# A gather's scaled sums moved from the vector engine to matmuls in column quarters

## The chip, the cores and the metric

The kernel runs on one core of a Trainium2 chip. The metric is the time of a launch on the device in microseconds (us), the median of several runs. The profiler's own execution is told by its span, from the first instruction to the last.

## The reference, cut to what matters

Two layers work on 256 latent tokens and 256 context tokens of 1024 features. A layer mixes tokens (a chunked gated delta rule whose latent scan starts from the context's final state, a pooling mixer, a Fourier mixer), and then looks up experts:

```python
# PEER: 8 heads, 128 x 128 experts, 16 chosen per head and token
s_top, i_top = top_k(scores, 16)                 # by each of two halves of a key
best, pos = top_k(sums of pairs, 16)
idx  = key_0 * 128 + key_1                       # 8 x 16 = 128 experts of a token
gate = softmax(best)
act  = gelu(sum_d h[t, d] * expert_u[idx[t, k], d])
out[t] = sum_k gate[t, k] * act[t, k] * expert_v[idx[t, k]]
x = x + g2 * out
```

The last layer needs of the context only the states of its scans. So experts are looked up three times: for the context in the first layer, and for the latents in both. All data are float32.

## The kernel before, in words

The program is written in Python, unrolled, and handed to a planner that gives each of the engines a fixed order of instructions: what comes earlier in the program has priority, and an instruction that is ready may pass one that is not. Tiles come from pools with a tag and a number of buffers; a new tile of a tag waits until the one whose place it takes has been read for the last time. PSUM's eight banks are tags as well (`BANKS`, line 173): "pj0", "pj1", "c0", "c1", "c2", "s" once each and "po" twice. `using(...)` gives a stage other tags.

The order of the program is: modulation vectors; the context's columns, scan and update in the first layer; the choice of the context's experts (`gather_select`, line 910); a first part of fetching their rows (`gather_rows`, line 956); the latents' columns, scan, update and choice in the first layer; the latents' experts in the first layer (`stream`, line 1087); the last layer for the latents, which ends with a second `stream`.

The latents' lookups are dense. `stream` goes over 128 first keys. For each, `first(i)` loads a tile of u, splits it in two parts (ACT's copy, line 1100, and POOL's subtraction, line 231, called from 1101) and adds 24 matmuls of 128x256 to a bank "s" (lines 1111 to 1113); `second(i)`, 17 tiles behind, weights the activations with the gates, splits a tile of v, and adds 12 matmuls of 128x512 to four banks (line 1142). In the first layer the gates of 32 first keys at a time are built by `chunk` (line 1028): one-hot tiles on DVE, 768 small matmuls (line 1052), copies to SBUF.

The context's lookup is a gather. `gather_select` writes a head's 16 indices per token as soon as that head is chosen (line 939), tokens on partitions. `gather_rows` takes choice j of block b of 128 tokens: an indirect DMA from POOL's queue (line 966) brings for each token, on its own partition, one row of a table that holds u and v side by side, 2048 numbers or 8 KB. DVE multiplies the half of u with the token's features and sums (line 975; 19 of the 256 go to POOL and ACT, lines 972 and 973), ACT applies Gelu and the gate (lines 979 and 980), and DVE adds the half of v, scaled by that one number per token, to the block's sum (line 986):

```python
dve.scalar_tensor_tensor(acc, v, dots[:, i : i + 1], acc, op0=OP.mult, op1=OP.add)
```

The first 100 of 256 such steps stand ahead of the latents' first layer (lines 1193 to 1195) with four buffers of 8 KB for them, the others behind first key 114 of the stream (`KV`, lines 177 and 1239) with three, followed there by the context's residual and its columns and scan of the last layer (`context`, line 1220). Being late in the program, these steps fill in where an engine has nothing of higher priority.

Of the kernel before, what the change touches and what calls it, by code (L numbers as in the profile page):

```python
# [28 lines left out]
def _constants():  # L29
# [4 lines left out]
    # cumulative sums along the tokens of a chunk, forwards and backwards: [j, i]  # L34
# [5 lines left out]
    # masks are added to exponents' arguments: [token, token], nothing outside a chunk  # L40
# [40 lines left out]
def _tiles(w, width):  # L81
    """[1024, n] as [128, n / width, 8 / deep, deep * width], deep * width = 2048: a partition's share of a
    tile lies together, deep rows of 128 in it."""
    deep = 2048 // width
    n = w.shape[1]
    w = w.reshape(KT // deep, deep, 128, n // width, width).transpose(2, 3, 0, 1, 4)
    return np.ascontiguousarray(w.reshape(128, n // width, KT // deep, 2048))


def _columns(v):  # L90
    """[..., 128 n] as [128, ..., n]"""
    v = v.reshape(*v.shape[:-1], -1, 128)
    return np.ascontiguousarray(np.moveaxis(v, -1, 0))


def _layout(i):
# [25 lines left out]
    for l in range(depth):  # L122
# [9 lines left out]
        if l < depth - 1:  # L132
            a[f"uv{l}"] = np.concatenate([i["expert_u"][l], i["expert_v"][l]], 1)
        # a tile per first key: the rows of u transposed, and the rows of v
# [10 lines left out]
def _body(st, tc, a, out, dbg, until):  # L145
# [26 lines left out]
    # the banks of PSUM: three for projections, one for each of three chains, two that sum outputs  # L172
# [3 lines left out]
    KC, TC = 32, 8  # first keys of a chunk of gates, tokens at a time  # L176
    KV = 114
    KVC = 2
    roles = {"ring": None, "split": None, "lo": "pool", "sb": 2, "wb": 1}  # what a stage uses in place of its own tags of PSUM, and of the weights' ring
# [11 lines left out]
    class Stage:  # L191
        """tiles of a pool that is opened and closed by hand"""
# [11 lines left out]
    def bank(shape, tag):  # L204
        tag = roles.get(tag, tag)
        if tag == "pj":
            turns[0] += 1
            tag = f"pj{turns[0] % 2}"
        return pp.tile(shape, F32, tag=tag, bufs=BANKS[tag], name=nm(tag))
# [23 lines left out]
    def rsqrt(x, n, tag=""):  # L233
        """1 / sqrt(x) of [128, n] positive values, by Newton's steps."""
# [10 lines left out]
    def two_parts(x, hi, lo):  # L245
        """x as a sum of two parts that the tensor engine reads exactly in one pass each"""
        act.copy(hi, x)
        (pool_tt if roles["lo"] == "pool" else dve.tensor_tensor)(lo, x, hi.bitcast(F32), op=OP.subtract)
        return hi, lo

    def product(out, x, y, start, stop):
        """out += x^T y, of operands in one part, or in two: only the product of the two second ones drops out"""
# [4 lines left out]
    def wtile(name, *index):  # L257
        """2048 of a weight's columns as two tiles; a function of a row of 128 and the columns' width"""
# [15 lines left out]
    def modulation(l, vecs):  # L274
        """[128, 6, 8, stream]: modulation vectors, a feature per partition."""
        m = mods[l]
        for vec in vecs:
            for half in range(2):
                # quarter j of the partitions sums the rows k = j, j + 4 for the two streams
# [22 lines left out]
    def scales(l, which, m, s):  # L302
        """norm's weight times 1 + scale, and the shift: [128, 8] each"""
# [4 lines left out]
    def in_rows(vec, half, tag):  # L308
        """half of [128, 8] as a row of 512, the same on all partitions"""
# [10 lines left out]
    def normed(x, xn, tag, scratch=None):  # L320
        """xn = x / rms(x), by rows"""
# [7 lines left out]
    def transposed(xns, sc, sh, hT):  # L329
        """hT [128, 8, 256] = (xn * sc + sh) transposed"""  # L330
# [16 lines left out]
    def columns_by_feature(name, c, hs):  # L347
        """256 columns of a weight times hT: [128, 2, 256], a column per partition"""
# [10 lines left out]
    def columns_by_token(name, n, h):  # L359
        """512 columns of a weight times hT: a block's [128, 512] each, a token per partition"""  # L360
# [44 lines left out]
    def columns(l, s, m, full, keep, tl):  # L405
# [4 lines left out]
        else:  # the last use of X  # L410
# [13 lines left out]
        # gates of the delta rule: [token, block, 16]  # L424
# [16 lines left out]
        # softplus(z) = max(z, 0) + ln(1 + exp(-|z|))  # L441
# [24 lines left out]
        # factors by token: [beta, -beta exp(g), exp(g_end - g)]  # L466
# [6 lines left out]
        # decay of a whole chunk, on all partitions: [chunk, 8]  # L473
# [13 lines left out]
        def conv(part, hp):  # L487
            """silu of the short convolution for two heads: part 0, 1, 2 = q, k, v: [128, 2, 256]"""
# [15 lines left out]
        def by_token(part, tok, feat, norm_scale):  # L504
            """a part by token [128, 2, 4, 128] (and by feature [128, 4, 256]), each head's vector over its norm"""
# [39 lines left out]
        if full:  # L545
            # the remaining columns by token: the delta rule's gate | pooling | Fourier
# [63 lines left out]
    def scan(l, s, full, state, tl, chains=4):  # L610
# [9 lines left out]
        def prepare(i):  # L620
# [5 lines left out]
            # g by token, along the columns  # L626
# [21 lines left out]
            # (1 + L)^-1, from blocks of one row on, two blocks at a time  # L648
# [40 lines left out]
        for step in range(4):  # L689
# [3 lines left out]
            for d in range(2):  # L693
# [25 lines left out]
                if full:  # L719
                    # a chunk's bank sums both directions: started once, by its first product  # L720
# [13 lines left out]
    def update(l, s, m, state, po, tl):  # L734
# [3 lines left out]
        # output of the delta rule: normed, gated  # L738
# [27 lines left out]
    def select(l, sp, hs, pair, gates, groups, after=lambda h: None):  # L766
        """pair(h): the keys of a head's chosen experts, [128, block, 2, 16]; gates(h, n): the gates of n heads from
        h on, [128, block, n, 16]; groups: how many heads' gates are worked out at a time"""
# [49 lines left out]
        def by_pair(h, tv, ti):  # L818
            tif = sp("tif", [128, NB * 2, TOPK], 2, BF)
            act.copy(tif, ti.rearrange("p b i k -> p (b i) k"))  # L820
            # of the 16 x 16 sums only those can be chosen that fewer than 16 others precede in both orders:
            # all of rows 0 to 3, and four columns of the others
# [12 lines left out]
            # their rows and columns  # L835
# [19 lines left out]
            # and by those the keys  # L855
# [42 lines left out]
    def residual(l, s, m, accs):  # L898
        """X += g2 * accs, halves of [128, 512] by block"""
# [10 lines left out]
    def gather_select(l, s, m, rows, done):  # L910
        """the chosen experts and gates per token, for their rows to be fetched"""
        idx = rows("idx", [128, NB, HEADS * TOPK], 1, I32)
        gate = rows("gate", [128, NB, HEADS, TOPK])
        st = {}
        for b in range(NB):
            st["acc", b] = rows(f"acc{b}", [128, D])
# [19 lines left out]
        def after(h):  # L936
            if h == 0:
                by_token()
            dve.scalar_tensor_tensor(
                idx[:, :, h * TOPK : h * TOPK + TOPK], keys[0][:, :, 0], float(NKEYS), keys[0][:, :, 1],  # L940
# [3 lines left out]
        keys = [None]  # L944
        select(l, sp, (hT,), pair, lambda h, n: gate[:, :, h : h + n], GROUPS, after)
        for b in range(NB):
            st["h2", b], st["idx", b], st["gate", b] = h2[b], idx[:, b], gate[:, b]
            dump(f"idx{l}{s}{b}", st["idx", b])
            dump(f"gate{l}{s}{b}", st["gate", b])
        sp.close()  # L950
        return st

    GRP = 1
    GROUPS = (1, 2, 5)

    def gather_rows(l, s, m, rows, buffer, st):
        """the chosen experts' rows fetched per token, a group of them for all tokens of a block at a time"""
        for j0 in range(0, HEADS * TOPK, GRP):
            h = j0 // TOPK
            for b in range(NB):  # L960
                acc = st["acc", b]
                dots = rows("dots", [128, GRP], 4)
                uvs = []
                for i in range(GRP):
                    uv = buffer()
                    pool.indirect_dma_start(  # L966
                        out=uv, out_offset=None, in_=a[f"uv{l}"],
                        in_offset=bass.IndirectOffsetOnAxis(ap=st["idx", b][:, j0 + i : j0 + i + 1], axis=0),
                    )
                    uvs.append(uv)  # L970
                    if j0 >= PST and (j0 * NB + b) % PMOD == 0:
                        pool_tt(uv[:, 0:D], uv[:, 0:D], st["h2", b], op=OP.mult)
                        act.activation(uv[:, 0:D], uv[:, 0:D], AF.Copy, accum_out=dots[:, i : i + 1])
                    else:
                        dve.scalar_tensor_tensor(  # L975
                            uv[:, 0:D], uv[:, 0:D], 1.0, st["h2", b], op0=OP.mult, op1=OP.mult,
                            accum_out=dots[:, i : i + 1],
                        )
                act.activation(dots, dots, AF.Gelu)  # L979
                act.activation(dots, dots, AF.Copy, scale=st["gate", b][:, h, j0 % TOPK : j0 % TOPK + 1])  # L980
                for i in range(GRP):
                    v = uvs[i][:, D:]
                    if j0 + i == 0:
                        dve.tensor_scalar(acc, v, dots[:, i : i + 1], None, op0=OP.mult)
                    else:
                        dve.scalar_tensor_tensor(acc, v, dots[:, i : i + 1], acc, op0=OP.mult, op1=OP.add)  # L986
                yield
        residual(l, s, m, [[st["acc", b][:, n * 512 : n * 512 + 512] for n in range(2)] for b in range(NB)])

    TG, IG = 16, 8  # tokens of a group of gates, first keys of a group  # L990
    LAG = (17, 32)  # tiles of u ahead of tiles of v
    UVA, UVB, UVN = 3, 1, 100  # buffers of rows fetched, and more of them for the first ones
    PST, PMOD = 60, 7
# [3 lines left out]
    def dense_select(l, s, m, dp, side):  # L997
        """tokens by feature, in two parts, and the chosen experts' two keys and gates by choice"""
# [29 lines left out]
    def chunk(parts, c, make):  # L1028
        """the gates of a chunk of first keys: [second key, first key, token]"""
# [29 lines left out]
    def build(l, chosen, gdram, side):  # L1059
        """gates by expert: [second key, first key, token]"""  # L1060
# [242 lines left out]
```

## Time and profile before

| | |
|---|---|
| time of a launch | 3435.21 us, median of 3 runs (3434.55 to 3441.6) |
| profiled execution, span | 3421.3 us (its time outside the span is not in the profile; the runs' median is 13.9 us above the span) |
| PE busy | 2934.5 us, 86% of the span |
| DVE busy | 2721.9 us, 80% |
| POOL busy | 1658.3 us, 48% |
| ACT busy | 1407.8 us, 41% |
| DMA | 712.74 MB, of which 268.45 MB through the queue of the indirect DMAs |
| granted TensorE clock, mean | 0.916 of full speed |

Busy time is the time in which an instruction of the engine is in progress; a matmul's end is modelled, so a busy PE is not PE at its peak. A line such as L986 is that of the kernel before. A time on the left of a row counts from the first instruction. One fp32 matmul of the program leaves two records in the trace.

### The profile page before, as it was taken

What the parts mean: (1) busy time and instruction counts of PE and PEld (TensorE: products, weight loads), DVE (VectorE), ACT (ScalarE), POOL (GpSimd) and SP (SyncE); (2) the same over time, 40 slices, a digit from 0 to 9 for tenths busy, and PEclk for the clock granted to TensorE, in tenths of its full rate; (3) what the DMA queues carried; (4) which work ended last, traced back from release to release, by engine and by line L of the source; (5) the groups of instructions that cost most, each with busy time, mean ns of one, the idle gap of its engine ahead of it and who ended that gap; (6) DMA issues with size and microseconds to landing.
All of it is one profiled execution on the core that took longest, in us unless ns stands there. A gap on an engine that the chain in (4) does not pass through costs nothing. (4 is left out here: it accounts for less than half of the span.)

```text
span 3421.3 us, 51677 instructions
## 1 busy us (share of the span) xinstructions
PE 2934.5 (86%) x19512; PEld 2488.9 (73%) x19512; DVE 2721.9 (80%) x4617; ACT 1407.8 (41%) x2648; POOL 1658.3 (48%) x976
## 2 busy tenths in 40 slices
PE   7999946768497898898899799999776899999998
PEld 4687725636386787787788677878576788899997
DVE  4535999879999999999999976643399967777777
ACT  4533334222233443344344354643235834444443
POOL 0241237732555775777677542334256732344442
PEclk9999967879687997999899899999889999999999
DMA  6603875688666876877677653252243576666664
GB/s 249 221 26 133 334 287 211 225 345 297 233 222 240 288 252 216 283 258 268 235 275 267 227 185 114 70 174 87 65 127 111 185 245 204 198 211 212 211 209 136
DMA packets 192106, 712.74 MB, mean 208 GB/s; under 512 B 18544, under 2 KB 58864, under 8 KB 157040
## 3 DMA queue, kind: packets, MB, share of 16 engines
q1 hardware_dynamic: 154992, 440.98, 38.9%
q0 software_dynamic: 36864, 268.45, 21.7%
q8 instruction: 153, 2.51, 0.3%
q14 instruction: 97, 0.79, 0.1%
HBM read 690.49 MB, written 18.87 MB: 207 GB/s over the span
## 5 line engine op out<-in xcount | busy, mean ns | idle before, releaser
L231 POOL TENSOR_TENSOR lu<-w,hu 128x1024 fp32r<-128x1024 f32 x256 | 670.5, 2619 | 512.0 <-ACT hu L1100 498.1
L1111 PE MATMUL s<-Hh,hu 128*128 128x256 f32 x2048 | 607.9, 297 | 75.4 <-ACT we L1115 63.0
L1113 PE MATMUL s<-Hh,lu 128*128 128x256 f32 x2048 | 604.2, 295 | 21.3 <-POOL lu L231 20.7
L966 POOL DMA_INDIRECT uv<-in_uv,idx x256 | 378.1, 1477 | 483.1 <-DVE acc L986 265.7
L1112 PE MATMUL s<-Hl,hu 128*128 128x256 f32 x2048 | 596.7, 291 | 0.0
L1111 PEld LDWEIGHTS s<-Hh,hu 128*128 128x128 f32 x2048 | 411.6, 201 | 93.0 <-ACT we L1115 72.2
L1113 PEld LDWEIGHTS s<-Hh,lu 128*128 128x128 f32 x2048 | 410.4, 200 | 28.3 <-POOL lu L231 26.9
L986 DVE SCALAR_TENSOR_TENSOR acc<-uv,dots,acc 128x1024 f32<-128x1024 f32 x254 | 409.9, 1619 | 14.7 <-ACT dots L980 14.5
L1112 PEld LDWEIGHTS s<-Hl,hu 128*128 128x128 f32 x2048 | 409.9, 200 | 6.9 <-issue 0.4
L1101 DVE TENSOR_TENSOR lv<-w,hv 128x1024 fp32r<-128x1024 f32 x256 | 356.3, 1392 | 59.6 <-ACT hv L1100 58.4
L1100 ACT CAST hu<-w 128x1024 fp32r<-128x1024 f32 x256 | 268.0, 1047 | 277.0 <-PE s L1112 206.6
L1131 DVE TENSOR_TENSOR we<-we,g 128x256 f32<-128x256 f32 x128 | 258.4, 2034 | 145.0 <-ACT we L1115 126.0
L975 DVE SCALAR_TENSOR_TENSOR uv<-uv,h 128x1024 f32<-128x1024 f32 x237 | 349.6, 1477 | 14.7 <-DMA uv<-in_uv,idx 14.5
L1100 ACT CAST hv<-w 128x1024 fp32r<-128x1024 f32 x256 | 267.9, 1046 | 213.8 <-PE pj L1142 169.3
L1052 PE MATMUL c<-og,two 128*128 128x32 bf16 x3072 | 234.5, 243 | 59.2 <-DVE og L1046 56.6
L1052 PEld LDWEIGHTS <-two 128*128 128x128 bf16 x3072 | 209.1, 160 | 95.0 <-issue 47.4
L979 ACT ACTIVATE dots<-dots 128x1 f32<-128x1 f32 x256 | 51.8, 203 | 519.1 <-DVE uv L975 518.5
L231 POOL TENSOR_TENSOR wl<-we,wh 128x256 fp32r<-128x256 f32 x128 | 146.5, 1146 | 122.9 <-ACT wh L1133 73.2
L1142 PE MATMUL po<-lv,wh 128*128 128x512 f32 x512 | 172.2, 418 | 29.5 <-DVE lv L1101 28.8
L1142 PE MATMUL po<-hv,wh 128*128 128x512 f32 x512 | 167.1, 407 | 15.7 <-ACT hv L1100 8.8
L231 POOL TENSOR_TENSOR C<-L,levels 128x512 f32<-128x512 f32 x96 | 135.2, 1424 | 86.9 <-PE c L665 38.1
L1142 PE MATMUL po<-hv,wl 128*128 128x512 f32 x512 | 164.3, 402 | 3.3 <-POOL wl L231 3.3
(427 smaller groups left out, 6433.3 us busy)
## 6 DMA issues: line engine op xcount, KB each, us to landing
w<-in_tab SPq DMA_DIRECT2D x512, 512.0 KB, 4.5
w<-in_wmod SPq DMA_DIRECT2D x96, 512.0 KB, 5.1
w<-in_wq SPq DMA_DIRECT2D x48, 512.0 KB, 4.6
w<-in_win SPq DMA_DIRECT2D x44, 512.0 KB, 4.7
gd<-gs SPq DMA_DIRECT2D x16, 1024.0 KB, 4.3
g<-gd SPq DMA_DIRECT2D x16, 1024.0 KB, 5.8
w<-in_wrest SPq DMA_DIRECT2D x24, 512.0 KB, 3.8
w<-in_wout SPq DMA_DIRECT2D x24, 512.0 KB, 4.9
```

The costliest lines, as they stand in the source:

```text
L231: pool.tensor_tensor(out, x, y, op=op)
L966: pool.indirect_dma_start(out=uv, out_offset=None, in_=a[f"uv{l}"], in_offset=bass.IndirectOffsetOnAxis(ap=st["idx", b][:, j0 + i : j0 + i ...
L975: dve.scalar_tensor_tensor(uv[:, 0:D], uv[:, 0:D], 1.0, st["h2", b], op0=OP.mult, op1=OP.mult, accum_out=dots[:, i : i + 1],)
L986: dve.scalar_tensor_tensor(acc, v, dots[:, i : i + 1], acc, op0=OP.mult, op1=OP.add)
L1052: pe.matmul(p[:, t1 - t0 + t], two[:, :, t], og[:, i, :, t], start=(i == 0), stop=(i == 2))
L1100: act.copy(hi, raw)
L1101: eng(lo, raw, hi.bitcast(F32), op=OP.subtract)
L1111: pe.matmul(p, hi[:, ks], Hh[:, k], start=(k == 0), stop=False)
L1112: pe.matmul(p, hi[:, ks], Hl[:, k], start=False, stop=False)
L1113: pe.matmul(p, lo[:, ks], Hh[:, k], start=False, stop=(k == KT - 1))
L1131: dve.tensor_tensor(wt, wt, g, OP.mult)
L1142: pe.matmul(acc[b][n], x[:, ts], y[:, n * 512 : n * 512 + 512], start=(i == 0 and j == 0), stop=(i == NKEYS - 1 and j == 2),)
```

## The change

The table of u and v side by side becomes two tables. The steps of a block are no longer tied together choice by choice:

- `scores(b)`: for each of 128 choices, an indirect DMA brings the tokens' rows of u (4 KB each), and DVE multiplies and sums, now for all 256. Then Gelu and the gates are applied to the whole 128 x 128 tile at once, and it is transposed: choices on partitions, tokens along the columns.
- `sums(b)`: for each of 128 tokens, an indirect DMA brings the rows of v of that token's 128 choices, one choice per partition; the indices for that are a transposed copy (`idx_t`). The sum over choices is a matmul: the stationary operand is a tile of 32 columns, zero but for one column with the token's 128 weights, the moving one 512 columns of the rows. Tokens go in pairs (g = 0, 1), halves of the features in two (n = 0, 1), and these four matmuls write the four quarters of 32 partitions of one bank, over 32 pairs. Then ACT copies the bank, and two DMAs from ACT's queue bring the halves to the place of the block's features.
- Order: scores of block 0; scores of block 1 with the sums of block 0 in turn; sums of block 1. The first 384 steps (`EARLY`: all but the sums of block 1) stand ahead of the latents' first layer, the others behind first key 8 of the stream (`REST`). The context's columns and scan stay behind first key 114. Five buffers of 4 KB hold the rows.
- The indices are gathered as floats head by head and copied to integers after the last head.
- Banks: the early part uses "s", the rest "c2". The modulation with vector 5 moves ahead of the context's update, and that of the last layer's vectors 1 and 0 uses "c2" where it used "s".

```diff
-            a[f"uv{l}"] = np.concatenate([i["expert_u"][l], i["expert_v"][l]], 1)
+            a[f"u{l}"], a[f"v{l}"] = i["expert_u"][l], i["expert_v"][l]
...
+        if tag == "vb":
+            tag = "s"
...
-                idx[:, :, h * TOPK : h * TOPK + TOPK], keys[0][:, :, 0], float(NKEYS), keys[0][:, :, 1],
+                idx_f[:, :, h * TOPK : h * TOPK + TOPK], keys[0][:, :, 0], float(NKEYS), keys[0][:, :, 1],
...
+        dve.tensor_copy(idx, idx_f)
+        p = bank([128, T], "c2")
+        for b in range(NB):
+            pe.transpose(p[:, b * 128 : b * 128 + 128], idx_f[:, b], ident)
+        dve.tensor_copy(idx_t, p)
...
+    def gather_rows(l, s, m, rows, st):
+        pairs, half = 32, 64
+        wz = rows("wz", [128, half, pairs])
+        pool.memset(wz, 0.0)
+        spots_of = wz.rearrange("p (g r) c -> p g (r c)", g=2)[:, :, 0 : pairs * pairs : pairs + 1]
+        w_t = {}
+
+        def fetch(table, index):
+            t = rows("uv", [128, D], ROWS)
+            pool.indirect_dma_start(
+                out=t, out_offset=None, in_=a[f"{table}{l}"], in_offset=bass.IndirectOffsetOnAxis(ap=index, axis=0)
+            )
+            return t
+
+        def scores(b):
+            dots = rows("dots", [128, HEADS * TOPK])
+            for j in range(HEADS * TOPK):
+                u = fetch("u", st["idx", b][:, j : j + 1])
+                dve.scalar_tensor_tensor(
+                    u, u, 1.0, st["h2", b], op0=OP.mult, op1=OP.mult, accum_out=dots[:, j : j + 1]
+                )
+                yield
+            act.activation(dots, dots, AF.Gelu)
+            dve.tensor_tensor(dots, dots, st["gate", b].rearrange("p h k -> p (h k)"), OP.mult)
+            p = bank([128, 128], "vb")
+            pe.transpose(p, dots, ident)
+            w_t[b] = rows(f"w_t{b}", [128, 128])
+            act.copy(w_t[b], p)
+
+        def sums(b):
+            for q in range(128 // half):
+                t0 = q * half
+                dve.tensor_copy(spots_of, w_t[b][:, t0 : t0 + half].rearrange("p (g r) -> p g r", g=2))
+                p = bank([128, 512], "vb")
+                for r in range(pairs):
+                    vs = []
+                    for g in range(2):
+                        t = b * 128 + t0 + g * pairs + r
+                        vs.append(fetch("v", st["idx_t"][:, t : t + 1]))
+                        if g == 0:
+                            yield
+                    for n in range(2):
+                        for g in range(2):
+                            o = 32 * (2 * n + g)
+                            pe.matmul(
+                                p[o : o + 32], wz[:, g * pairs + r], vs[g][:, n * 512 : n * 512 + 512],
+                                start=(r == 0), stop=(r == pairs - 1), tile_position=(0, o),
+                            )
+                    if r < pairs - 1:
+                        yield
+                o = rows("sum", [128, 512], 2)
+                act.copy(o, p)
+                for n in range(2):
+                    act.dma_start(
+                        st["h2", b][t0 : t0 + half, n * 512 : n * 512 + 512], o[n * half : n * half + half]
+                    )
+                yield
+
+        yield from scores(0)
+        first = sums(0)
+        for _ in scores(1):
+            yield
+            next(first)
+            yield
+        for _ in first:
+            yield
+        yield from sums(1)
...
+    ROWS, EARLY = 5, 384
...
-        modulation(0, (2, 4, 3))
+        modulation(0, (2, 4, 3, 5))
...
-    for _ in range(UVN):
+    for _ in range(EARLY):
         next(fetching)
...
-    with using(c2="s", pj="s"):
-        modulation(0, (5,))
...
-    with using(c2="s", pj="po"):
+    with using(pj="po"):
         modulation(1, (1, 0))
...
+    with using(vb="c2"):
+        sums = stream(0, keys, Hh, Hl, su, sv, LAG[0], {REST: fetch_rest, KV: context})
```

## Rows read from the trace of the kernel before

**Rows 1.** The page, busy tenths of DVE in 40 equal slices.
```profile
DVE  4535999879999999999999976643399967777777
```

**Rows 2.** Table by stretches: length, each engine's busy time (instructions), clock, DMA.
```profile
core 0: us, PE busy (x) PEld busy (x) DVE busy (x) ACT busy (x) POOL busy (x), PEclk, DMA share, GB/s
440.00:890.00 450.00, 298.84 (x1458) 213.58 (x1456) 409.57 (x991) 133.34 (x373) 217.62 (x146) 0.77 0.75 277
890.00:2115.00 1225.00, 1059.19 (x7937) 929.02 (x7938) 1115.29 (x1235) 509.35 (x978) 782.42 (x428) 0.90 0.70 239
2115.00:2400.00 285.00, 274.15 (x2040) 227.18 (x2040) 151.15 (x277) 131.91 (x261) 119.82 (x97) 1.00 0.33 105
```

**Rows 3.** Groups by cost: busy us, mean ns; idle time before.
```profile
L986 DVE SCALAR_TENSOR_TENSOR acc<-uv,dots,acc 128x1024 f32<-128x1024 f32 x254 | 409.9, 1619 | 14.7 <-ACT dots L980 14.5
```

**Rows 4.** Line 939: min/median/max ns, first and last start.
```profile
L939 DVE SCALAR_TENSOR_TENSOR idx<-pair x8: 170/182/193, 329.0 to 502.0; 128x32 int32<-128x32 f32 x8
```

**Rows 5.** Stretch tables of line 986, then of line 975.
```profile
300.00:500.00 200.00, 36.79 (x27) 0.87 0.77 285
890.00:2115.00 1225.00, 253.23 (x149) 0.90 0.70 239
...
300.00:500.00 200.00, 38.46 (x61) 0.87 0.77 285
890.00:2115.00 1225.00, 199.92 (x256) 0.90 0.70 239
```

**Rows 6.** Line 966: the fetch's ns, and us to its landing.
```profile
L966 POOL DMA_INDIRECT uv<-in_uv,idx x256: 932/1676/4374, 329.5 to 1969.0; - x128
...
DMA to landing us min/median/max: 5.5/7.4/13.6
```

**Rows 7.** POOL in order of time: start, length.
```profile
680.51 1.74 POOL L966 DMA_INDIRECT uv<-in_uv,idx  x1 [3.23 <-DVE acc L986]
682.55 0.93 POOL L966 DMA_INDIRECT uv<-in_uv,idx  x1 [0.30 <-issue]
```

**Rows 8.** DVE in order of time beside them.
```profile
678.96 2.48 DVE L986 SCALAR_TENSOR_TENSOR acc<-uv,dots,acc 128x1024 f32<-128x1024 f32 x2
681.35 1.22 DVE L975 SCALAR_TENSOR_TENSOR uv<-uv,h 128x1024 f32<-128x1024 f32 x1
```

**Rows 9.** Stretch tables of POOL's lines 966, then 231.
```profile
440.00:890.00 450.00, 125.23 (x89) 0.77 0.75 277
...
440.00:890.00 450.00, 92.40 (x57) 0.77 0.75 277
```

**Rows 10.** Table by stretches, the busiest 40 us of DMA.
```profile
720.00:760.00 40.00, 27.66 (x72) 13.09 (x70) 29.59 (x50) 8.31 (x25) 15.88 (x11) 0.90 1.01 400
```

**Rows 11.** Tile s between 440 and 900 us.
```profile
L284 PE MATMUL s<-w,cvec x32: 592/1060/1063, 448.9 to 469.3; 128*32 128x512 f32 x32
```

**Rows 12.** Lines 1111 and 1142 in the first layer's stream.
```profile
L1111 PE MATMUL s<-Hh,hu x1024: 275/283/584, 890.2 to 2038.3; 128*128 128x256 f32 x171
...
L1142 PE MATMUL pj<-hv,wl x256: 386/395/632, 1071.8 to 2115.5; 128*128 128x512 f32 x128
```

**Rows 13.** Stretch tables of lines 1111, then 1142, last layer's stream.
```profile
3000.00:3400.00 400.00, 160.80 (x568) 108.39 (x568) 1.00 0.63 202
...
3000.00:3400.00 400.00, 207.41 (x846) 154.00 (x845) 1.00 0.63 202
```

**Rows 14.** PE in order of time, gates of a chunk.
```profile
1200.34 0.70 PE L1052 MATMUL c<-og,two 128*128 128x32 bf16 x8
1200.86 0.71 PE L1142 MATMUL po<-hv,wh 128*128 128x512 f32 x2
```

**Rows 15.** PE in order of time, matmuls in column quarters.
```profile
2311.23 1.92 PE L284 MATMUL s<-w,cvec 128*32 128x512 f32 x16
2313.08 0.66 PE L661 MATMUL pj<-ident,Xi 128*128 128x128 f32 x4
```

**Rows 16.** Line 255 between 2040 and 2115 us.
```profile
L255 PE MATMUL c<-hT,w x128: 377/380/383, 2053.1 to 2096.9; 128*128 128x256 f32 x128
```

More of the change, by code (lines that the diff above doesn't have):

```diff
@@ L176, in _body @@
     KC, TC = 32, 8
-    KV = 114
+    KV, REST = 114, 8
     KVC = 2
@@ L912, in gather_select @@
         idx = rows("idx", [128, NB, HEADS * TOPK], 1, I32)
+        idx_t = rows("idx_t", [128, T], 1, I32)
         gate = rows("gate", [128, NB, HEADS, TOPK])
         st = {}
-        for b in range(NB):
-            st["acc", b] = rows(f"acc{b}", [128, D])
         sc, sh = scales(l, 1, m, s)
@@ L944, in gather_select @@
         keys = [None]
+        idx_f = sp("idx_f", [128, NB, HEADS * TOPK])
         select(l, sp, (hT,), pair, lambda h, n: gate[:, :, h : h + n], GROUPS, after)
+        dve.tensor_copy(idx, idx_f)
[3 more added lines that the diff above has]
+        dve.tensor_copy(idx_t, p)
         for b in range(NB):
@@ L949, in gather_select @@
             dump(f"gate{l}{s}{b}", st["gate", b])
+        st["idx_t"] = idx_t
         sp.close()
         return st
-    GRP = 1
     GROUPS = (1, 2, 5)
[L956 to L968, printed above, removed]
-                    )
[L970 to L986, printed above, removed]
-                yield
-        residual(l, s, m, [[st["acc", b][:, n * 512 : n * 512 + 512] for n in range(2)] for b in range(NB)])
@@ new lines, in gather_rows @@
+    def gather_rows(l, s, m, rows, st):
[50 more added lines that the diff above has]
+                        st["h2", b][t0 : t0 + half, n * 512 : n * 512 + 512], o[n * half : n * half + half]
+                    )
+                yield
+        yield from scores(0)
[7 more added lines that the diff above has]
+        yield from sums(1)
+        residual(l, s, m, [[st["h2", b][:, n * 512 : n * 512 + 512] for n in range(2)] for b in range(NB)])
@@ L990, in _body @@
     TG, IG = 16, 8
     LAG = (17, 32)
-    UVA, UVB, UVN = 3, 1, 100
-    PST, PMOD = 60, 7
+    ROWS, EARLY = 5, 384
     OHB = (4, 10)
@@ L1178, in _body @@
     rows = Stage("rows")
-    steady, extra = Stage("uv"), Stage("uv")
     cw = Stage("select_weights")
@@ L1183, in _body @@
     cw.close()
-    def buffer():
-        n = buffer.n
-        buffer.n += 1
-        if n < UVN and n % (UVA + UVB) >= UVA:
-            return extra("uv", [128, 2 * D], UVB)
-        return steady("uv", [128, 2 * D], UVA)
-    buffer.n = 0
-    fetching = gather_rows(0, CTX, m, rows, buffer, chosen)
-    for _ in range(UVN):
+    fetching = gather_rows(0, CTX, m, rows, chosen)
+    for _ in range(EARLY):
         next(fetching)
-    extra.close()
     lk, lc = Stage("keep", "right"), Stage("columns", "right")
@@ L1223, in context @@
             pass
-        steady.close()
         rows.close()
@@ L1237, in context, with fetch_rest @@
         ck.close()
-    sums = stream(0, keys, Hh, Hl, su, sv, LAG[0], {KV: context})
+    def fetch_rest():
+        for _ in fetching:
+            pass
+    with using(vb="c2"):
+        sums = stream(0, keys, Hh, Hl, su, sv, LAG[0], {REST: fetch_rest, KV: context})
     with using(c2="s"):
```

## The prediction, made before the change was run

> **What bounds the kernel now.** I read the page's busy slices first: DVE is at nine tenths or more in all but two of the slices 5 to 23 (of 85.5 us each) and nowhere else for long [rows 1]. The table by stretches then gives the stages. From 440 to 890 us DVE is busy 409.6 of 450 while PE has 298.8; in the first layer's stream, 890 to 2115, DVE has 1115.3 of 1225, PE 1059.2, POOL 782.4; from 2115 to 2400 PE has 274.2 of 285 [rows 2]. So DVE sets the pace up to 2000 and PE after it, and PE's 1059 is no proof of a full engine: an isolated matmul's record is long, so I price PE below by spacings. The groups by cost show what the change takes from DVE: 254 scaled additions, 409.9 us [rows 3]. On the other side 256 fetches of a row of u and v together become 512 of half the size, and PE gets 512 matmuls.
>
> The decisive question is not what DVE gets rid of but what now has to come before what. Two orders are new. The indices are copied as a whole when all eight heads are chosen, so the first fetch waits for the last head; and the early sums lie in PSUM bank "s", which the stream's score tiles need, so the stream's first matmul waits until all 384 early fetches have been consumed.
>
> **Start of the fetches.** Now the first of eight writes of the indices ends at 329 us and a fetch follows at once; the last begins at 502.0 [rows 4]. Between 300 and 500 the gather takes 36.8 + 38.5 = 75 us of DVE [rows 5]; without it the choosing would end near 502 - 75 = 427. I take 440, between that and 502 (nothing gained).
>
> **The early 384 fetches.** Each brings 128 rows of 4 KB, 0.524 MB. Three resources bound their pace.
> POOL: a fetch lasts at least 0.93 us, its median is 1.68 [rows 6]. The rows beside each other show why: the one at 680.51 starts inside an addition on DVE (678.96, two together 2.48 us, ending 681.44) and lasts 1.74; the next, at 682.55, starts as DVE's product from 681.35 ends, 0.30 us after the fetch before it, and takes 0.93 [rows 7, 8]. So 0.93 + 0.30 = 1.24 us undisturbed and 1.74 + 0.30 = 2.04 behind a DVE instruction over 1024 elements. The 256 products that stay (1.22 us, rows 8) hold DVE for 312 us, some 45% of the time it will take: 1.24 + 0.45 x 0.80 = 1.60 us. POOL's other work in this part is now 92.4 us, in 57 instructions, and has to stay [rows 9]. Sum: 384 x 1.60 + 92 = 706 us, so the bank is free at 440 + 706 = 1146. Ends: 384 x 1.24 + 92 = 568 (1008) and 384 x 2.04 + 92 = 875 (1315).
> DMA: from 440 to 890 now 277 GB/s x 450 us = 125 MB move [rows 2], of which 89 fetches of 1.05 MB [rows 9] are 93; the other 32 MB are weights and stay. 201 + 32 = 233 MB are 583 us at 400 GB/s, the best stretch of 40 us here [rows 10], so the bank is free at 1023 at best; at 277 GB/s they are 841, so 1281.
> Buffers: five. A fetch now takes 5.5 us at least and 7.4 in the median until it lands [rows 6]; with 1.3 for the product and 0.3 until POOL goes on, 7.1 to 9.0 us round five buffers is 1.4 to 1.8 a fetch (half as many bytes land sooner; a buffer of v waits for its pair).
> I take POOL's 1146, which lies between the ends of all three (with its other work 1.84 us for each fetch).
>
> The Trainium skill, "SBUF — State Buffer", section "Who interferes with whom", has a rule against my 1.60: a tensor_tensor on DVE takes only the shared read interface, and descriptor generation needs the write interface, so (inferred there) it should not hold up such a fetch. Rows 7 and 8 differ, 1.74 against 0.93, and I go by them; by the rule the pace would be 1.24, which is the fast rival below.
>
> The latents' chain of the first layer now ends with the stream's first matmul at 890 [rows 12]. Its DVE, PE and POOL work is the same; it lies beside the fetches and, behind them in priority, ends later than now, but I expect not after 1146. A set of sums waits on PE, in order, for its two fetches, and queued behind it are the latents' matmuls, which have room until then. From about 900 on PE is then nearly idle. Bank "s" has users in this part today too, a modulation from 448.9 to 469.3 [rows 11]; the change moves it ahead, and another to bank c2, so that they don't wait.
>
> **The stream.** Its PE time, from spacings. A tile: in the last layer's stream 568 records of line 1111 (8 a tile) and 846 of line 1142 (12) in 400 us are 71 tiles, 5.65 us each, with PE full [rows 13]; 128 tiles are 723 us. Gates: 8 matmuls of line 1052 take from 1200.34 to 1200.86, 0.065 us each [rows 14]; 768 for a chunk are 50 us, and of the four chunks the first is worked out while the bank is awaited, leaving 150. The sums of the second block: a pair of tokens makes four matmuls in four column quarters, eight records. The same form exists: 16 records of line 284 start at 2311.23 and the next matmul at 2313.08 [rows 15], so 0.92 us for eight; 64 pairs are 59 us (as much again, of the first block, lies in the early part, where PE has room). The context's columns that share the stretch now: 128 records from 2053 to 2097, 44 us [rows 16]. Together 723 + 150 + 59 + 44 = 976 us.
> What else it needs is less: DVE loses its 453 us of gather from 1115 (253 + 200, rows 5), leaving 662; POOL keeps 128 fetches where it has 146. Wait by wait, what is late next is PE. At the 96% that it reaches from 2115 to 2400 (rows 2) 976 becomes 1017 us. Ends: 976, and 1050 at 93%, if the 128 fetches, which come first in priority, hold up the splitting on POOL.
>
> **Sum.** 1146 + 1017 = 2163 where the stretch now ends at 2115.5 [rows 12]: 48 us later. From there on nothing changes, PE being the bound as before. The moved modulation adds 0 to 10 us to the context's scan; I take nothing, its matmuls fit between the scan's. ACT loses 512 small instructions and waits for nothing new that matters. Copies of the sums, a transpose and eight small DMAs from ACT's queue are under 10 us in all and lie beside fetches. The profiled span is 3421.3 and the runs' median 3435.2 lies 13.9 above it: 3421 + 48 = 3469, in a run 3483 us.
>
> **Rivals.**
> Fetches at DMA pace (faster): if DVE's products don't hold up POOL, DMA is the bound and the bank is free at 1023; 1023 + 1017 = 2040, 75 us earlier: 3360. For it: 400 GB/s has been seen, and DVE will be idle half the time. Against: the median fetch of 1.68, and that no fetch may want for a buffer. It decides below 1.71 us a fetch all told. The Trainium skill's rule on the shared read interface, weighed above, would bring this about; rows 7 and 8 speak against it.
> The five buffers and the order on PE set the pace (much slower): a v fetch gives its buffer back when its pair has come and PE, in order, has reached the set; at 2.04 us a fetch plus POOL's 92 the bank is free at 1315; the stretch then ends at 2332, 217 later: 3652. It decides once a round of the five buffers takes longer than 5 x 1.84 = 9.2 us.
> Quarters not side by side: four times 0.92 us a pair, 64 x 2.76 = 177 us more in the stream: 3660. Rows 15 speak against it.
> Both effects cancel: the time stays within 0.2% (7 us, about what can be told apart here) if the bank is free near 1098, 1.71 us a fetch with POOL's other work.
>
> **Chances.** Forecast, slower by 0.2 to 4%: 0.42. DMA pace and all of its neighbourhood that ends faster: 0.36. Cancelling: 0.08. Buffers: 0.10. Quarters: 0.04. So faster 0.36, same 0.08, slower 0.56. The likeliest case alone reaches from 3442 to 3560. Taking in most of the fast case, the range is 3350 to 3575; it leaves out the far end of that case and most of the slow one, 2 in 10.
>
> **What would show it.** Right: no indirect DMA before some 430 us; the 384th near 1140; line 1111's first matmul right behind it, hundreds of us later than 890, with PE little busy and its clock lowered before it; then PE near full to some 2160, DVE around 60%. The two additions' lines gone; a set of quarters at 0.9 us. Wrong: the stream starting before 1050, or a stream longer than 1070 us though DVE is free (then PE waits for fetches), or the latents' selection, not the bank, as what the first matmul waits for.

## The result and the profile after

The changed kernel takes 3741.24 us (median of 4 runs, 3729.35 to 3743.77) where the kernel before takes 3437.14 beside it: 1.0888 times as long, 95% interval [1.0863, 1.0913]. Slower was forecast, but by 1.4%, and the time lies far outside the range. The profiled span went from 3421.3 to 3727.6 us, +306.3.

The table by stretches of the kernel after, cut where its stages now end (columns as in [rows 2]):

```profile
440.00:890.00 450.00, 321.58 (x1679) 222.54 (x1677) 366.42 (x979) 86.92 (x179) 294.77 (x223) 0.81 0.75 256
890.00:1325.40 435.40, 256.33 (x1137) 64.93 (x1136) 173.99 (x312) 16.65 (x17) 240.10 (x222) 0.50 0.79 266
1325.40:2450.30 1124.90, 1118.77 (x7871) 908.18 (x7872) 593.34 (x655) 462.00 (x664) 580.72 (x404) 0.97 0.56 184
```

Against [rows 2] there is a stage that did not exist: 435 us in which no engine is busy 60% of the time and the granted clock is 0.50, the lower of the two levels (1.2 of 2.4 GHz). Behind it the stream runs with PE busy 99% of the time, DVE 53%: DVE was relieved as meant, and PE is the bound.

Lines of the kernel after: the fetch (975, was 966 in [rows 6]), the sets of quarters (1011), the stream's first matmul (1156, was 1111 in [rows 12]); columns as in [rows 4].

```profile
L975 POOL DMA_INDIRECT uv<-in_u,idx x256: 935/941/3692, 438.8 to 1314.6; - x128
L975 POOL DMA_INDIRECT uv<-in_v,idx_t x256: 935/952/6104, 762.1 to 1759.8; - x128
...
L1011 PE MATMUL s<-uv,wz x512: 592/1061/1063, 782.2 to 1323.7; 128*32 128x512 f32 x171
...
L1156 PE MATMUL s<-Hh,hu x2048: 274/283/583, 1325.5 to 3705.5; 128*128 128x256 f32 x187
```

The first fetch starts at 438.8. The last matmul into bank "s" starts at 1323.7 and the stream's first at 1325.5, directly behind it: the bank is the gate. A fetch itself takes 0.94 us on POOL in the median, where [rows 6] had 1.68, and from 440 to 1325 us POOL is busy 535 of 885 us: over the whole early part it is not the bound. How many start when, from the stretch table of line 975 (length, POOL's busy time on it, count; then clock, DMA share, GB/s):

```profile
440.00:762.00 322.00, 171.59 (x128) 0.82 0.72 244
762.00:890.00 128.00, 37.12 (x37) 0.79 0.80 287
890.00:1325.00 435.00, 239.71 (x221) 0.50 0.79 266
```

That is 2.52, 3.46 and 1.97 us for each fetch. In the first stretch POOL is busy 237 us, 66 of them with other work than fetches, and its largest wait is for a buffer that DVE's products give back (engine, line, what it waited for: us in total, times, longest):

```profile
POOL uv L975 <- DVE uv L984: 44.1, 30, 5.0
```

In the second the latents' choosing has DVE (busy 122.7 of 128 us), and the products wait in line behind it with their buffers. In the third only the gather runs, once the first chunk of gates is through by some 980 us. Its waits from 1000 to 1160 us:

```profile
PEld s L1011 <- DMA uv<-in_v,idx_t: 147.2, 41, 4.7
...
DVE uv L984 <- DMA uv<-in_u,idx: 68.4, 30, 4.3
POOL uv L975 <- PE s L1011: 37.6, 21, 2.5
```

PE and DVE wait for rows to land, and POOL waits for a buffer back: a ring of five, whose round is the pace. The same stretch in the table of all engines:

```profile
1000.00:1160.00 160.00, 82.03 (x174) 7.87 (x168) 52.88 (x86) 1.87 (x2) 91.57 (x85) 0.50 0.83 282
```

85 fetches in 160 us are 1.88 us each, with DMA engines busy 83% of the time.

PE in order of time inside the stream shows the other surprise:

```profile
1452.25 1.06 PE L1011 MATMUL c<-uv,wz 128*32 128x512 f32 x6
1453.24 0.72 PE L1187 MATMUL po<-hv,wh 128*128 128x512 f32 x2
...
1456.22 1.05 PE L1011 MATMUL c<-uv,wz 128*32 128x512 f32 x2
1457.20 0.39 PE L1156 MATMUL s<-Hh,hu 128*128 128x256 f32 x1
```

The eight records of a set (the four matmuls of a pair of tokens) don't stand together as in [rows 15]. The first quarter, two records, needs only the first of the two fetches; PE's order puts it apart from the other six, with stream matmuls between. Two records hold PE for 0.98 us (1456.22 to 1457.20), six for 0.99: a bundle (records of a set that stand together) has a price, whatever its number of records. A set costs 1.97 us, not 0.92.

The 306 us by the prediction's own terms: the gate opens 179 us later than forecast (1325 for 1146), the stretch lasts 108 more (1125 for 1017), the rest of the kernel is 28 shorter than before (1277.3 for 1305.8, since part of the context's scan now lies inside the stream), and 48 were forecast: 179 + 108 - 28 + 48 = 307.

### The profile page after: what moved, and what is told of

It is laid out like the page before. It is cut to its first block, busy times and chain, and to the rows that moved or that the text cites. A ratio compares the mean times of both kernels' runs of the same rounds, so it can differ in the third digit from the quotient of the medians.

```text
span 3727.6 us, 53597 instructions
## 1 busy us (share of the span) xinstructions
PE 3244.1 (87%) x20540; PEld 2515.8 (67%) x20540; DVE 2303.1 (62%) x4407; ACT 1292.9 (35%) x2095; POOL 1724.5 (46%) x1214
## 5 line engine op out<-in xcount | busy, mean ns | idle before, releaser
L233 POOL TENSOR_TENSOR lu<-w,hu 128x1024 fp32r<-128x1024 f32 x256 | 626.3, 2447 | 698.4 <-ACT hu L1145 687.5
L1146 DVE TENSOR_TENSOR lv<-w,hv 128x1024 fp32r<-128x1024 f32 x256 | 337.1, 1318 | 190.7 <-ACT hv L1145 190.5
L1011 PE MATMUL s<-uv,wz 128*32 128x512 f32 x512 | 235.8, 1024 | 195.5 <-DMA uv<-in_v,idx_t 193.9
L975 POOL DMA_INDIRECT uv<-in_u,idx x256 | 296.1, 1157 | 216.4 <-DVE uv L984 70.6
L975 POOL DMA_INDIRECT uv<-in_v,idx_t x256 | 279.8, 1093 | 241.0 <-PE c L1011 88.4
L1011 PEld LDWEIGHTS s<-uv,wz 128*32 128x32 f32 x512 | 24.0, 137 | 362.3 <-DMA uv<-in_v,idx_t 355.0
L1176 DVE TENSOR_TENSOR we<-we,gs 128x256 f32<-128x256 f32 x128 | 158.5, 1269 | 172.4 <-ACT we L1160 159.8
L1082 DVE TENSOR_TENSOR two<-parts,spots 128x1024 bf16<-128x1024 bf16 x128 | 162.8, 1272 | 153.0 <-PE c L1097 144.6
L1097 PE MATMUL c<-og,two 128*128 128x32 bf16 x3072 | 217.6, 241 | 6.1 <-DVE og L1091 6.1
L233 POOL TENSOR_TENSOR wl<-we,wh 128x256 fp32r<-128x256 f32 x128 | 122.5, 959 | 119.5 <-ACT wh L1178 68.0
```

The source lines that it names most:

```text
L233: pool.tensor_tensor(out, x, y, op=op)
L975: pool.indirect_dma_start(out=t, out_offset=None, in_=a[f"{table}{l}"], in_offset=bass.IndirectOffsetOnAxis(ap=index, axis=0))
L1011: pe.matmul(p[o : o + 32], wz[:, g * pairs + r], vs[g][:, n * 512 : n * 512 + 512], start=(r == 0), stop=(r == pairs - 1), tile_position=( ...
L1097: pe.matmul(p[:, t1 - t0 + t], two[:, :, t], og[:, i, :, t], start=(i == 0), stop=(i == 2))
L1146: eng(lo, raw, hi.bitcast(F32), op=OP.subtract)
L1176: dve.tensor_tensor(wt, wt, g, OP.mult)
```

## Experiments

Theory: the gate (bank "s" behind 384 fetches at the pace of five buffers) and the split sets cost nearly all of it. Rivals: POOL's descriptor work or the fetches' bytes set the time, or the records themselves do.

**e1_bank: the gate taken away.** The first stream's scores lie in bank c2, and the sums of both blocks in "s"; the context's columns and scan, which used c2, go to "s" too.

```
-        scores = bank([128, 2, T], "s")
+        scores = bank([128, 2, T], "s" if l else "c2")
...
-    with using(vb="c2"):
+    with using(c2="c2"):
```

> The first layer's stream keeps its scores in bank c2 and not in s, so it no longer waits for the early sums; the later sums and the context's banks take s instead of c2. Theory (the wait for the bank is the main cost): the latents' selection and the first chunk of gates are done by 985 us, so line 1156's first matmul (1136 + 20 in the changed kernel) starts near 990 instead of 1325, and the stream with the 42 early sets still open then (1.97 us each, 83 us) ends near 990 + 1125 + 83 = 2200 instead of 2450: a launch near 3490 us, between 3430 and 3560. Rival (the gather's own pace of 2.3 us a fetch is the bound, whichever bank it uses): PE then waits, in order, for fetches inside the stream, the last fetch lands no earlier than now (1760) and the launch stays above 3640 us.

3530.82 us, ratio 1.0293 [1.0268, 1.0317]: 210 us of the loss were the gate, net of the early sets that now lie in the stream. The stream begins at 862.6, earlier than in [rows 12]:

```profile
L1157 PE MATMUL c<-Hh,hu x1024: 274/283/583, 862.6 to 2086.2; 128*128 128x256 f32 x171
```

Now some 120 sets lie in the stream, 1.97 us each, and it ends at 2132.5, 17 us later than before the change.

**e2_seven: seven buffers for the early fetches**, the bank as in the change.

```
-            t = rows("uv", [128, D], ROWS)
+            t = extra("uv", [128, D], 2) if n < EARLY and n % 7 >= 5 else rows("uv", [128, D], ROWS)
```

> Seven buffers of rows for the 384 early fetches where the changed kernel has five; bank s as there. Theory (a round of the buffers sets the early pace, 5 x 2.30 = 11.5 us): the pace where nothing but the gather runs (1000 to 1325, 1.89 us a fetch) falls towards what the DMA engines can do (280 GB/s at a busy share of 0.83 is 337 GB/s, 1.56 us), the stream starts 60 to 130 us earlier than 1325, and the launch takes 3610 to 3680 us. Rival (POOL, or the order in which PE waits, sets it): pace and start stay within 2%, 3700 to 3750 us.

3639.9 us, ratio 1.0603 [1.0574, 1.0631]. The gate opens at 1166.7, 159 us earlier, with POOL's work and the bytes the same. The stretch of above, in this kernel:

```profile
1000.00:1160.00 160.00, 100.29 (x230) 10.48 (x230) 69.30 (x113) 0.00 (x0) 120.05 (x114) 0.56 0.99 369
```

114 fetches instead of 85, DMA 0.99 busy instead of 0.83, 369 GB/s instead of 282. So the five buffers set the pace there; with seven, DMA does. Ahead of it 148 and 54 fetches start in the first two stretches of the table above, which had 128 and 37, but there the comparison is not clean. The latents' layer runs later in this kernel: a load of its weights (line 428, on SP's queue) waits for the copy of the indices.

```profile
SPq L428 <- DVE idx L948: 37.3, 1, 37.3
```

The context's choosing is through earlier, and the first fetch starts at 411.4, so 27 of the 159 us are an earlier start. And the first chunk of gates, worked out from 875 us on in the changed kernel, begins at 1171.4 and lies in the stream, which lasts 1195.6 us instead of 1124.9; so the launch gains less, 101 us.

**e3_early128: only 128 fetches ahead of the stream** (bank and five buffers as in the change).

```
-    ROWS, EARLY = 5, 384
+    ROWS, EARLY = 5, 128
```

> Only the 128 score fetches of the first block stand ahead of the latents' first layer; the other 384 fetches come behind the stream's eighth key, with their sums in bank c2, so nothing early holds bank s. Theory (bank): the stream starts by 990 us at the latest, probably near 900, and then PE carries all 128 sets (252 us at 1.97 us) and DVE 128 products: 900 + (976 - 59 + 252) / 0.96 = 2118, a launch of 3400 to 3520 us. Rival (pace): the fetches take as long as now, the stream is held up by them, above 3640 us.

3518.81 us, ratio 1.0245 [1.0215, 1.0274], at the upper edge of what was expected. The stream begins at 827.7. It is the gate again, removed in another way: fewer fetches before it.

**e4_firsthead: the integer indices written head by head**, as in the kernel before; a float copy stays for the transposes.

```
+            dve.scalar_tensor_tensor(
+                idx[:, :, h * TOPK : h * TOPK + TOPK], keys[0][:, :, 0], float(NKEYS), keys[0][:, :, 1],
+                op0=OP.mult, op1=OP.add,
+            )
...
-        dve.tensor_copy(idx, idx_f)
```

> Each head's indices are written as integers at once, as the kernel before did, so the score fetches of block 0 can start behind the first head (329 us) instead of behind the last (439). Theory (the end of the early fetches sets the stream's start): some 30 fetches move into the 110 us won, at 2.3 us each the stream starts 50 to 90 us earlier, and the launch takes 3650 to 3690 us. Rival (latents' work or something else sets the start): within 0.5% of the changed kernel, 3722 to 3760 us.

3687.13 us, ratio 1.0746 [1.0719, 1.0773]. The first fetch starts at 333.8, 105 us earlier, and the stream at 1277, only 48 earlier. By 440 us 32 fetches have started, 3.4 us each, with DVE busy 105.6 of those 110 us, much of it with the other heads; at the 1.97 us that a fetch takes at the end that lead is worth 63 us, of which 48 are left.

**e5_bundle: e1 with one bundle a set.** The quarter that waits for the later fetch goes first, the others directly behind it.

```
+                    last = quarter(0, 1)
+                    with tc.issue_after(getattr(last, "ins", last)):
+                        quarter(0, 0)
+                        quarter(1, 0)
+                        quarter(1, 1)
```

> The free-bank kernel (first stream's scores in c2, the sums in s), and in every set the quarter that waits for the later of the two fetches (n = 0, g = 1) is issued first, with the other three queued directly behind it. Theory (a set costs by its bundles, not by its records): the set's records stand together as one bundle of 8 at 0.92 to 1.0 us, where the free-bank kernel has two bundles, 0.98 and 0.99 us; some 120 sets lie in the stream, so about 117 us go: 3413 us (3395 to 3440). Rival (the stream is paced by the fetches, or the set costs by its 8 records): the set still takes 1.9 us or the time turns into waits for uv, and the time stays at 3510 to 3540 us.

3455.42 us, ratio 1.0069 [1.0046, 1.0092]: between the two ranges, a miss for both. The price itself came as expected, eight records in 0.99 us (PE in order of time):

```profile
1462.47 1.06 PE L1010 MATMUL s<-uv,wz 128*32 128x512 f32 x8
1463.46 0.38 PE L1164 MATMUL c<-Hh,lu 128*128 128x256 f32 x1
```

Between 900 and 2150 us the sets take 132 us where they took 249 in e1, so 116 went, and the stream ends 76 earlier (2056.6 for 2132.5). The other 40 turned into waits between the stream's own instructions: from 870 us to the stream's end PE is idle 17 us in e1 and 59 in e5. The largest of PE's waits there, first of e1 and then of e5:

```profile
PE c L1098 <- DVE og L1092: 9.1, 7, 3.8
...
PE s L1011 <- DMA uv<-in_v,idx_t: 1.6, 1, 1.6
```

```profile
PE c L1103 <- DVE og L1097: 31.9, 18, 4.1
PE s L1010 <- DMA uv<-in_v,idx_t: 8.8, 9, 2.5
PE po L1193 <- POOL wl L233: 5.1, 4, 2.1
```

With less to do PE overtakes DVE, above all where DVE makes the gates of a chunk.

**e6_bundle_only: the same edit on the changed kernel**, gate and all.

> The changed kernel as it is (bank s still gates the stream), with only the order of the quarters changed: (0, 1) first, the other three directly behind it. Theory: the 64 sets in the stream lose one bundle each, 64 x 0.99 = 63 us; ahead of the stream the 64 sets lose one bundle of 1.9 us at the lower clock, which shortens the buffers' round by at most that, 0 to 120 us in 560. Expected 3640 us (3590 to 3685). Rival (the bundles don't count): 3725 to 3745 us.

3658.77 us, ratio 1.0668 [1.065, 1.0686], within the range. The gate hardly moves (1316.5 for 1325.5: ahead of it PE is not the bound), and the stream shortens from 1125 to 1066 us, 59 where 63 were worked out.

**e7_half: e1 with the features' second half left out of the sums**, so each set has two quarters and half the records.

```
-                    for n in range(2):
+                    for n in range(1):
                         for g in range(2):
```

> The free-bank kernel with the second half of the features (n = 1) left out of the sums: two quarters a set instead of four, the fetches unchanged. Theory (a bundle has its price whatever its number of records): the set is still two bundles, of 2 and 2 records, 0.98 us each, and the time is that of the free-bank kernel, 3530 us (3510 to 3540). Rival (price by record, 8 records in 1.97 us): half of 1.97 us goes in each of some 120 sets, 118 us: 3412 us (3390 to 3440).

3545.88 us, ratio 1.0345 [1.0324, 1.0367]; e1 was 1.0293. Half the matmuls are gone and no time with them; it is 15 us more, 6 above the range expected (the stream begins 6 us later and lasts 8 longer), and I don't know of what. In order of time every set is two bundles of two records, 0.98 us each:

```profile
1450.44 1.05 PE L1011 MATMUL s<-uv,wz 128*32 128x512 f32 x2
1451.42 0.50 PE L1188 MATMUL po<-hv,wl 128*128 128x512 f32 x1
...
1454.02 1.04 PE L1011 MATMUL s<-uv,wz 128*32 128x512 f32 x2
1455.00 0.39 PE L1159 MATMUL c<-Hh,lu 128*128 128x256 f32 x1
```

The price by record is refuted: two quarters or one cost what four cost, if they don't stand together.

**e8_three: e5 with the indices head by head.**

> Free bank and one bundle a set as in the kernel of that, and besides the integer indices written head by head, so that the fetches start about 105 us earlier (333.8 instead of 438.8 us in the run that had this alone). Theory (once the stream has begun TensorE's own work sets the end): some 25 to 30 more sets are over before the stream begins, at about 1 us each, so 15 to 45 us less than the kernel with free bank and bundles: 3385 us (3360 to 3420). Rival (fetches set the end of the stream): up to 105 us less, 3300 to 3360 us.

3410.7 us, ratio 0.9946 [0.9929, 0.9963]: faster than the kernel before. It takes 45 us off e5, the upper end of what was expected, though its stream (897 to 2095.4) begins 37 us later and lasts as long. What moves is the context. Its columns (line 257, [rows 16] before) need all the sums; in e1 and e5 they come behind the stream (it ends at 2132.5 and 2056.6), in e8 inside it. The three in this order:

```profile
L257 PE MATMUL s<-hT,w x128: 379/379/793, 2142.7 to 2181.7; 128*128 128x256 f32 x128
```

```profile
L257 PE MATMUL s<-hT,w x128: 379/379/793, 2063.8 to 2103.3; 128*128 128x256 f32 x128
```

```profile
L257 PE MATMUL s<-hT,w x128: 377/379/395, 1974.0 to 2019.0; 128*128 128x256 f32 x128
```

From the stream's end to the end of the span it is 1397.5 us in e1, 1395.1 in e5 and 1312.1 in e8; 1305.8 before. (In e3 the columns lie behind the stream too, from 2159.8, and it is 1399.3.) That also explains why e1, its stream only 17 us later than before the change, is still 109 us longer: 17 + 92.

**e9_buffers: e8 with two more buffers for the first 192 fetches.**

> The kernel of three edits (free bank, one bundle a set, indices head by head) with two more buffers for the first 192 fetches. Theory (what is left over the kernel before is the fetches that are still to come when the stream begins, and their pace before it is the round of five buffers): some 190 fetches lie ahead of the stream in the kernel of three edits; with seven buffers a fetch took 2.02 us in the mean instead of 2.3, so 25 to 35 more are over by then, the last one comes 60 to 100 us earlier, and a part of it, as in the step from two to three edits (101 us earlier gave 45 us), comes off the end: 3380 us (3350 to 3410). Rival (from there on TensorE's work alone sets the end): no change, 3400 to 3420 us.

3491.49 us, ratio 1.0183 [1.0167, 1.0199]; wrong in sign, and no test of the theory. The last fetch did start 124 us earlier than in e8 (1775 for 1898), but the load of the latents' weights (line 428, on SP's queue) now stood behind the choosing of the heads, for which it doesn't wait in e8, and the stream began at 991.3 instead of 896.9. Both kernels with two more buffers have this wait (e2 and e9), and neither the changed kernel nor e8 has it; that the buffers took the space which the load needs is argued from that, not shown.

```profile
SPq L428 <- DVE idx_f L944: 91.7, 1, 91.7
```

**e10_order: e8 with EARLY = 500.**

> The kernel of three edits with EARLY = 500 instead of 384: the steps of nearly all fetches are written out ahead of the latents' layer, so that they come first where the order leaves a choice. Theory (the pace of the fetches inside the stream, 3.0 to 3.75 us each, comes from the place of the sets in TensorE's order): an earlier end of the fetches and 0 to 40 us less, 3370 to 3415 us. Rival (the order brings them as early as the buffers allow anyway): 3400 to 3420 us.

3407.12 us, ratio 0.9933 [0.9916, 0.9951]. Its stream (893.7 to 2103.3) and last fetch (1905 for 1898) are as in e8 (896.9 to 2095.4): the order of writing changes nothing that can be told apart.

**e11_again: e8 a second time.**

> The kernel of three edits once more, beside the other two, to see by how much it is below the kernel before: 3411 us, ratio 0.992 to 0.997.

3409.2 us, ratio 0.9945 [0.993, 0.996]. So the change with its three costs taken away is 0.5% faster than the kernel before.

## Why the prediction was wrong

- **Start of the fetches: right.** 438.8 for 440, and e4 shows it to be the whole copy of the indices.
- **The gate: right in kind.** The stream's first matmul follows the last early sum by 1.8 us; PE is at the lower clock before it, as said, though busy 59% of the time and not little. e1 and e3 remove it in two ways.
- **The early fetches' pace: wrong, the first failed step.** "I take POOL's 1146", 1.84 us for each fetch: it was 2.3. POOL's own price was near: a fetch held it 1.16 us in the mean, where the prediction has 1.30 (1.60 without the 0.30 between fetches), and its other work took 86 us for 92, nearly all of it in the first two stretches of the table. Against 1.60 us a fetch and POOL's other work where it lies (66, 20 and 0 us) the three stretches cost 51, 48 and 81 us more. What failed is the buffers' term, 1.4 to 1.8, which left out the queues in which a buffer's holders stand. From 1000 us on the ring alone is left: 1.88 us, a round of 9.4, just above the 9.2 from which the prediction's own rival decides, and e2 shows the ring to be the cause. In the first two DVE serves the latents' chain as well. The prediction let that chain run behind the fetches and end late; it ran among them, and its gates began at 875 us. That the products standing in line behind it held the buffers is read from the waits; no run takes the chain away. The rival of the five buffers put the gate at 1315 and had a chance of 0.10.
- **POOL's price: right.** Rows 7 and 8 were read rightly. Of the early fetches 149 start inside a product and last 1.45 us in the mean, and 142 of them end 0.7 to 1.0 us behind the product's end; the 260 of all 512 that start while DVE is idle last 0.94 us in the median and 1.12 at most. In e8 55 fetches start inside a tensor_tensor, that of line 1155 which splits a tile of v (128x1024), and last 1.69 us in the median. The Trainium skill's rule weighed there ("SBUF — State Buffer", "Who interferes with whom"), by which such a fetch should not be held up, does not agree with these rows. For the time it decided nothing, since POOL was not the bound. One fetch inside a product, in order of time:

```profile
475.42 1.22 DVE L984 SCALAR_TENSOR_TENSOR uv<-uv,h 128x1024 f32<-128x1024 f32 x1
475.77 1.68 POOL L975 DMA_INDIRECT uv<-in_u,idx  x1 [0.82 <-DVE uv L984]
```

- **The quarters: wrong, the second failed step.** "0.92 us for eight" is the price of eight records that stand together, and e5 has it (0.99). The prediction saw that a quarter waits for its fetch, but did not see that the first quarter waits for another fetch than the rest and so gets another place in PE's order: 1.97 us, 67 us more over 64 sets. e6 takes 59 of them back, e7 shows that the records don't matter.
- **The stream: near, by terms that miss both ways.** By the spacing of PE's records the 1125 us are 782 for the tiles (723 in the prediction), 144 for the gates (150), 121 for the sets (59), 73 for the context's columns and what came forward of its scan (44), and 6 of waiting (41, the 4% allowed). So beside the sets the tile was mis-sized: 6.1 us, not the 5.65 of the last layer's stream; why, stays open (the mean granted clock was 0.97).
- **The rest: "nothing changes" nearly held (28 us shorter), and by luck.** Where the fetches reach into the stream's end (e1, e5), the context falls behind it and costs some 90 us.
- **DMA pace: no.** The best 40 us of the early part moved 368 GB/s, not 400. With seven buffers DMA was the bound (369 GB/s, e2), and the gate still opened at 1167, not 1023.

## What to carry to other kernels

Price a gather through a ring of buffers by its round, with every holder of the buffer in it (landing, the partner it waits for, the consumer's place in a queue shared with other work), and ask what opens only when the last one is through. Column quarters are cheap only if nothing can come between them: let the one whose input comes last be issued first, and chain the rest to it. When a bank or a buffer gates a long stage, look for another bank before tuning what fills it.

## What the runs showed of the hardware

A lone fp32 matmul over 512 columns in one quarter of the columns (2 records) held PE for 0.98 us at full clock, four of them side by side 0.99. Fetches of 128 rows of 4 KB moved 282 GB/s from five buffers and 369 from seven, the DMA engines 0.83 and 0.99 busy. A fetch held POOL 0.94 us; where it started inside a DVE instruction that reads two tiles of 128x1024 fp32 numbers, it mostly ended some 0.8 us behind that instruction's end.
